# A two-layer streaming encoder step on one core: where the dense products of a head stand against the outputs of the head two back

## The chip, the cores and the metric

The program runs on one core of one Trainium2 chip. The metric is the device time of one execution in microseconds (us); the time before is the median of three runs. The profile is of one further execution.

## What is computed

The reference runs 1024 prompt frames and 32 frames of a running stream through two layers of width 1024. The change touches only the first mixer, a gated linear recurrence with 8 heads of width 128 and chunks of 64 frames:

```python
q, f, i, g = jnp.split(h @ w_in, 4, axis=-1)
forget = lbf + (1.0 - lbf) * jax.nn.sigmoid(f.astype(F32))
...
o_inter = jnp.einsum('blhk,bhkv->blhv', q * jnp.exp(b), S)
scores = jnp.einsum('btshk,bshk->bhts', decay * q[:, :, None], k)
o_intra = jnp.einsum('bhts,bshv->bthv', scores, v)
S_new = jnp.exp(b_last)[..., None] * S + jnp.einsum('bshk,bshv->bhkv', k * jnp.exp(b_last[:, None] - b), v)
...
o = rms_norm(o, g_norm) * jax.nn.silu(g.astype(F32)).reshape(B, T, A_HEADS, A_DV)
return o.reshape(B, T, D_MODEL).astype(h.dtype) @ w_out, S
```

Then x becomes x + rms_norm(mix), which is normalised again for the feed-forward part that follows.

## The kernel before

The 1056 frames are cut into three blocks of 384, 384 and 288 columns (`BL`). A block's activations lie as 8 tiles of 128 features by its columns, each split into a high and a low part (`xh`, `xl`); a weight unit of 128x1024 (`wunit`) is loaded by a DMA into `wst` (2 buffers), rounded to `wh` by ACT (L102) and its remainder put into `wl` by DVE (L103), 4 buffers each. A dense product is 24 matmuls: 8 feature tiles times three pairs of parts, in `mm_fm` (L133, weights stationary, up to 384 columns) or in `mm_tm` (L145, frames stationary, 256 columns). `mmps` gives PSUM banks from a ring of 4.

The loop over blocks b and heads h is a pipeline three units deep; a unit is one head of one block, and there are 24. In the iteration of unit c, `p1` is the unit before and `p2` the one two back. The source order of an iteration is: `stage_a` (forget and query products of c, and their evictions L756 to L764), in between them `states(p2)` (transposes `pt`, products `pu`, then the states `Sq` by DVE L947, or by ACT L945 for the first chunk); `stage_c(p1)` (the scores `psA`, `psB`, and the masked copies of them into `at`); `outputs(p2)` (the products `po`, L970 from `at` and values, L973 from `Q` and the states; then a copy and three squares on ACT into `ssq`); the list `fill[h]`; and `stage_b(c)` (the decayed products on DVE, POOL and ACT that end with `Q64` and `K64`, 2 buffers each).

In `fill`, even heads hold `vproj` (two wunits and 3 dense products for the values of a pair of heads, 72 matmuls at L145, evicted by ACT L708). Odd heads from 3 on hold `gproj` (the same for the gate of the pair whose second head `outputs` has just made: `rsqrt` of `ssq` on DVE, 10 small instructions, then the products, and evictions L725, L726, L729). At h = 1 of blocks 1 and 2 `gproj(3, b - 1)` is followed by `oback(b - 1)`, which transposes all heads' outputs (`pgt`) and splits them (L992, L993).

`fill` also advances the generators `OP[b]` by steps. A generator is `outproj` (8 steps, each one output tile `mixb`: 24 matmuls, and two scaled wunits in every second step) and then `postnorm`: step 9 is `rnorm` (one matmul pair L180, then six DVE and four ACT instructions up to `rb2`), step 10 nothing, steps 11 to 14 two feature tiles each (per tile: L243 and L244 on DVE, a square on ACT, an add into `acc` on POOL, a DMA that loads `xo` and, per step, one that stores `mixb`). For block 0 step 15 is a second `rnorm`, step 16 nothing, and steps 17 and 18 load four stored tiles each, scale them (L274) and split them (`put_x`, L209, L210). Before the change `OP[0]` stands at h = 2, 3, 4, 6 of block 1 with two steps each, and in block 2 at h = 0 (2 steps), 1 (4 steps), 4, 5, 6, 7 (one each). `OP[1]` has two steps at h = 2, 3, 4 of block 2.

Each engine has its own queue of instructions. Their order is set when the program is built: by source order, except where the builder's own estimate has a later instruction ready sooner.

Of the kernel before, what the change touches and what calls it, by code (L numbers as in the profile page):

```python
# [8 lines left out]
F32 = mybir.dt.float32  # L9
# [50 lines left out]
def build(nc, tc, I, O):  # L60
    ctx = ExitStack()
    mult, add, sub, mn = ALU.mult, ALU.add, ALU.subtract, ALU.min
# [73 lines left out]
    def mm_tm(ps, rows, units, xh, xl, t0):  # L136
        n = 24
        i = 0
        for u, (wh, wl) in enumerate(units):
            for k in range(4):  # L140
                h, l = wh[:, k * 256:k * 256 + 256], wl[:, k * 256:k * 256 + 256]
                kt = u * 4 + k
                a, b = xh[:, kt, t0:t0 + rows], xl[:, kt, t0:t0 + rows]
                for (x, w) in ((a, h), (b, h), (a, l)):
                    last_mm[0] = nc.tensor.matmul(ps[:rows, :256], x, w, start=i == 0, stop=i == n - 1)  # L145
                    i += 1
# [5 lines left out]
    def rsqrt(dst, ss, v, t, u, cnt, sq, lin):  # L152

        lin(v, ss, 1.0 / cnt, EPS)
        nc.vector.tensor_scalar(dst.bitcast(I32), v.bitcast(I32), -0.5, float(0x5f3759df), mult, add)
        sq(t, dst)
        nc.vector.tensor_tensor(t, t, v, mult)
        lin(u, t, 0.375, -1.25)
        nc.vector.tensor_tensor(t, u, t, mult)
        nc.vector.scalar_tensor_tensor(dst, t, 1.875, dst, add, mult)  # L160
        sq(t, dst)
        nc.vector.scalar_tensor_tensor(t, t, -0.5, v, mult, mult)
        nc.vector.scalar_tensor_tensor(dst, t, 1.5, dst, add, mult)
# [434 lines left out]
    V, KE = nc.vector, nc.gpsimd  # L598
# [46 lines left out]
    def run(g):  # L645
        for _ in g or ():
            pass

    def go(g, n=1):
        for _ in range(n):  # L650
            next(g, None)

    with tc.tile_pool(name="hp", bufs=1) as hp, \
# [42 lines left out]
        vts, o_raw, ssq, r_o = {}, {}, {}, {}  # L696
# [15 lines left out]
        def gproj(p, b):  # L712
            units = wpair(I["wg"], p)
            W = BL[b][1]
            ro = hp.tile([128, 6], F32, tag="ro", name="ro", bufs=2)
            nv, nt, nu = [hp.tile([128, 6], F32, tag=t, name=t, bufs=2) for t in ("nv", "nt", "nu")]
            rsqrt(ro, ssq[p, b], nv, nt, nu, 128, lambda o, x: V.tensor_tensor(o, x, x, mult),
                  lambda o, x, m, a: V.tensor_scalar(o, x, m, a, mult, add))
            for jl in range(3):
                rows = min(128, W - jl * 128)  # L720
                ps = mmps()
                mm_tm(ps, rows, units, xs[b][0], xs[b][1], jl * 128)
                sg = hp.tile([128, 256], F32, tag="sg", name="sg", bufs=2)
                rc = rts[b][:rows, jl:jl + 1]
                nc.scalar.activation(sg[:rows], ps[:rows, :256], AF.Sigmoid, scale=rc)  # L725
                V.scalar_tensor_tensor(sg[:rows], ps[:rows, :256], rc, sg[:rows], mult, mult)  # L726
                for i in range(2):
                    o = o_raw[2 * p + i, b][:rows, jl, :]
                    V.scalar_tensor_tensor(o, sg[:rows, i * 128:i * 128 + 128], ro[:rows, 3 * i + jl:3 * i + jl + 1],  # L729
                                           o, mult, mult)  # L730
# [177 lines left out]
        def states(c):  # L908

            h, b, n = c["h"], c["b"], c["n"]  # L910
            hc = (h % 2) * 128
            vt = vts[h // 2, b]
            K64 = c["K64"]
            chunks = [(q, 128, c["D128"][:, q:q + 1]) for q in range(n)]
            if b == 2:
                chunks.append((2, 32, c["D64"][:, 4:5]))
                S0 = hp.tile([128, 128], F32, tag="S", name="S", bufs=2)
                nc.sync.dma_start(S0, I["state"][h])
            pt = hps.tile([128, 512], F32, tag="hs", name="pt", bufs=1)
            kT = hp.tile([128, 3, 128], F32, tag="kT", name="kT", bufs=1)  # L920
            for (q, rows, _) in chunks:
                nc.tensor.transpose(pt[:rows, q * 128:q * 128 + 128], K64[:, q * 128:q * 128 + rows], ident)
            kTf = kT.rearrange("p a b -> p (a b)")
            nc.scalar.copy(kTf[:, :n * 128], pt[:, :n * 128])
            if b == 2:
                nc.scalar.copy(kTf[:32, 256:384], pt[:32, 256:384])
            yield
            pu = hps.tile([128, 512], F32, tag="hs", name="pu", bufs=1)
            for (q, rows, _) in chunks:
                nc.tensor.matmul(pu[:, q * 128:q * 128 + 128], kT[:rows, q], vt[:rows, q, hc:hc + 128],  # L930
                                 start=True, stop=True)
            S = state[h]
            c["S"] = before = []
            for (q, rows, dcol) in chunks:
                j = 3 * b + q
                pq = pu[:, q * 128:q * 128 + 128]
                if j == 8:
                    S = S0
                before.append(S)
                if q == 2 and j < 8:  # L940
                    new = hp.tile([128, 128], F32, tag="state", name="state", bufs=10)
                else:
                    new = hp.tile([128, 128], F32, tag="Sq", name="Sq", bufs=5)
                if j == 0:
                    nc.scalar.copy(new, pq)  # L945
                else:
                    V.scalar_tensor_tensor(new, S, dcol, pq, mult, add)  # L947
                if j == 7:
                    nc.sync.dma_start(O["st_p"][h], new)
                if j == 8:  # L950
                    nc.sync.dma_start(O["st_s"][h], new)
                S = new
            state[h] = S
# [29 lines left out]
        def oback(b):  # L983
            W = BL[b][1]
            oh, ol = os[b] = newx(b)
            for h in range(8):
                pt = hps.tile([128, 512], F32, tag="hsc", name="pgt", bufs=2)
                for jl in range(3):
                    rows = min(128, W - jl * 128)
                    nc.tensor.transpose(pt[:, jl * 128:jl * 128 + rows], o_raw[h, b][:rows, jl, :],  # L990
                                        ident[:rows, :rows])
                nc.scalar.copy(oh[:, h, :], pt[:, :W])  # L992
                V.tensor_tensor(ol[:, h, :], pt[:, :W], oh[:, h, :].bitcast(F32), sub)  # L993
# [4 lines left out]
        OP = [op0(b) for b in range(NB)]  # L998
        p1 = p2 = None
        xld = None  # L1000
        for b in range(NB):
            fill = {h: [] for h in range(8)}
            for p in range(4):
                fill[2 * p].append(lambda p=p, b=b: go(v0 if p == b == 0 else vproj(p, b), 4))
                if p < 3:
                    fill[2 * p + 3].append(lambda p=p, b=b: gproj(p, b))
            if b > 0:
                fill[1].append(lambda b=b: (gproj(3, b - 1), oback(b - 1)))
                o = OP[b - 1]
                for h in (2, 3, 4):  # L1010
                    fill[h].append(lambda o=o: go(o, 2))
                if b == 1:
                    fill[6].append(lambda o=o: go(o, 2))
            if b == 2:
                for h, n in ((0, 1), (1, 2), (4, 1), (5, 1)):
                    fill[h].insert(0, lambda n=n: go(OP[0], n))
                for h, n in ((0, 1), (1, 2), (6, 1), (7, 1)):
                    fill[h].append(lambda n=n: go(OP[0], n))
            for h in range(8):
                c = {}  # L1020
                ga = stage_a(c, h, b)
                gs = states(p2) if p2 is not None else iter(())
                go(ga)
                go(gs)
                go(ga)
                go(gs)
                if p1 is not None:
                    stage_c(p1)
                if p2 is not None:
                    outputs(p2)  # L1030
                for f in fill[h]:
                    f()
                stage_b(c)
                p2, p1 = p1, c
                if xld is not None:
                    go(xld)
                if b + 1 < NB and h == 3:
                    xld = xload(b + 1)
                    go(xld)
# [4 lines left out]
        stage_c(p1)  # L1044
        outputs(p2)
        run(states(p1))
        outputs(p1)
        gproj(3, 2)
        go(OP[1])
        oback(2)  # L1050
    mb2c, mbs[2] = pool("mb0b", "right")
# [127 lines left out]
    with tc.tile_pool(name="aps", bufs=1, space=PSUM, reuse_waits="tile") as aps:  # L1179
# [148 lines left out]
        p, o = OP[0], OP[1]  # L1328
# [134 lines left out]
```

## Time and the profile before

| | |
|---|---|
| median of 3 runs | 2586.18 us (2575.33 to 2587.52) |
| profiled execution | 2586.45 us |
| its span, first to last instruction | 2584.7 us |
| mean granted TensorE clock | 0.98 |
| busy: PE, PEld, DVE, ACT, POOL | 96%, 92%, 66%, 43%, 17% |

The first mixer's loop fills the span from about 8 us to 640 us. The iterations of block 0 start at 7.7 us, those of block 1 at 185 us, those of block 2 at 399 us; one takes 20 to 30 us. In the rows, PE is TensorE's matmuls, PEld its weight loads, SPq the queue that issues DMAs; "idle before" is the time in which an engine stood still before an instruction, and the name behind the arrow is what ended it.

### The profile page before, as it was taken

How to read it: one execution, taken by the hardware profiler on the slowest of the kernel's cores; microseconds unless marked ns; L12 is line 12 of the kernel's file. 1: busy time of each engine (PE TensorE's matmuls, PEld its weight loads, DVE VectorE, ACT ScalarE, POOL GpSimd, SP SyncE). 2: the span in 40 equal slices, each digit the busy share in tenths (PEclk: the TensorE clock that was granted, in tenths of full speed). 3: DMA queues.
4: the chain of work that ended last, by engine and by line, in shares of the span. 5: the costliest groups of instructions: out<-in, count | busy, mean ns of one | idle time of the engine just before them, and what ended most of it. 6: DMA issues, size and time to landing. Idle time of an engine off the chain costs nothing.

```text
span 2584.7 us, 44049 instructions
## 1 busy us (share of the span) xinstructions
PE 2487.6 (96%) x17124; PEld 2387.2 (92%) x17124; DVE 1704.8 (66%) x3510; ACT 1104.9 (43%) x2395; POOL 444.7 (17%) x644
## 2 busy tenths in 40 slices
PE   7999998999999999999998999989999999999997
PEld 6999998998999999999998897758899999999996
DVE  8788679787876666553467647777876666652455
ACT  6555655655543333341344324556543333342332
POOL 4443434331300000000033321111300000000021
PEclk9999999999999999999999999989999999999998
DMA  5232333433522222242455542222522222252454
GB/s 172 87 99 93 119 105 124 129 125 97 163 81 81 75 75 77 83 165 79 145 171 157 169 138 68 73 78 95 159 75 87 75 75 75 77 174 75 149 171 144
DMA packets 124153, 287.98 MB, mean 111 GB/s; under 512 B 13432, under 2 KB 68632, under 8 KB 123944
## 3 DMA queue, kind: packets, MB, share of 16 engines
q1 hardware_dynamic: 123944, 285.17, 34.6%
q8 instruction: 134, 2.20, 0.4%
q14 instruction: 75, 0.61, 0.1%
HBM read 237.25 MB, written 48.07 MB: 110 GB/s over the span
## 4 chain that ended last, share of the span: by engine, by line
PE 61%; DVE 9%; DMA 4%; ACT 3%; issue 2%; POOL 0%; SPq 0%; POOLq 0%; DVEq 0%; ACTq 0%
PE mm L133 20%; PE mm L501 15%; PE mm L410 14%; PE c L410 6%; DVE wl L103 2%; PE mm L145 2%; PE sc L1227 1%; PE pav L1285 1%; ACT wh L102 1%; DMA wst<-in_wfo 1%; PE ptp L1267 1%; DVE xl L210 1%; DMA xl<-g 1%; DVE mix L244 1%; DVE wl L99 1%
## 5 line engine op out<-in xcount | busy, mean ns | idle before, releaser
L133 PE MATMUL mm<-xh,wh 128*128 128x384 f32 (+1 forms) x1968 | 632.9, 322 | 10.7 <-ACT xh L212 7.7
L133 PE MATMUL mm<-xh,wl 128*128 128x384 f32 (+1 forms) x1968 | 626.0, 318 | 7.9 <-DVE wl L103 5.5
L133 PE MATMUL mm<-xl,wh 128*128 128x384 f32 (+1 forms) x1968 | 627.3, 319 | 2.0 <-DVE xl L213 1.7
L174 POOL TENSOR_TENSOR acc<-acc,tmp 128x384 f32<-128x384 f32 (+1 forms) x168 | 204.0, 1219 | 1737.4 <-ACT tmp L173 1734.4
L103 DVE TENSOR_TENSOR wl<-wst,wh 128x1024 fp32r<-128x1024 f32 (+1 forms) x301 | 372.9, 1241 | 174.9 <-ACT wh L102 170.7
L102 ACT CAST wh<-wst 128x1024 fp32r<-128x1024 f32 (+1 forms) x301 | 313.8, 1046 | 370.5 <-PE mm L501 213.0
L133 PEld LDWEIGHTS mm<-xh,wh 128*128 128x128 f32 x1968 | 374.0, 190 | 17.6 <-ACT xh L212 8.0
L133 PEld LDWEIGHTS mm<-xh,wl 128*128 128x128 f32 x1968 | 374.2, 190 | 17.0 <-DVE wl L103 6.6
L133 PEld LDWEIGHTS mm<-xl,wh 128*128 128x128 f32 x1968 | 373.9, 190 | 11.2 <-DVE xl L213 5.1
L501 PE MATMUL mm<-xh,wl 128*128 128x384 f32 (+1 forms) x768 | 247.8, 323 | 3.2 <-DVE wl L103 3.2
L501 PE MATMUL mm<-xh,wh 128*128 128x384 f32 (+1 forms) x768 | 247.8, 323 | 1.3 <-ACT wh L102 1.3
L501 PE MATMUL mm<-xl,wh 128*128 128x384 f32 (+1 forms) x768 | 247.6, 322 | 0.0
L145 PE MATMUL mm<-wh,xh 128*128 128x256 f32 (+1 forms) x648 | 188.6, 291 | 0.8 <-ACT vt L708 0.8
L145 PE MATMUL mm<-wh,xl 128*128 128x256 f32 (+1 forms) x648 | 185.4, 286 | 0.0
L145 PE MATMUL mm<-wl,xh 128*128 128x256 f32 (+1 forms) x648 | 184.7, 285 | 0.0
L394 ACT CAST sh<-sr 128x512 fp32r<-128x512 f32 x144 | 89.5, 622 | 172.9 <-PE mm L410 146.8
L501 PEld LDWEIGHTS mm<-xh,wl 128*128 128x128 f32 x768 | 145.2, 189 | 3.9 <-DVE wl L103 3.9
L501 PEld LDWEIGHTS mm<-xh,wh 128*128 128x128 f32 x768 | 145.4, 189 | 1.5 <-ACT wh L102 1.5
L501 PEld LDWEIGHTS mm<-xl,wh 128*128 128x128 f32 x768 | 145.3, 189 | 0.0
L145 PEld LDWEIGHTS mm<-wh,xh 128*128 128x128 f32 (+1 forms) x648 | 120.5, 186 | 3.2 <-issue 1.7
L145 PEld LDWEIGHTS mm<-wh,xl 128*128 128x128 f32 (+1 forms) x648 | 120.5, 186 | 1.1 <-issue 0.3
L145 PEld LDWEIGHTS mm<-wl,xh 128*128 128x128 f32 (+1 forms) x648 | 120.4, 186 | 0.4
(283 smaller groups left out, 5144.3 us busy)
## 6 DMA issues: line engine op xcount, KB each, us to landing
wst<-in_wfo SPq DMA_DIRECT2D x92, 512.0 KB
wst<-in_wfi SPq DMA_DIRECT2D x88, 512.0 KB
wst<-in_wfq SPq DMA_DIRECT2D x47, 512.0 KB
g<-u SPq DMA_DIRECT2D x72, 192.0 KB
wst<-in_wi SPq DMA_DIRECT2D x24, 512.0 KB
wst<-in_wg SPq DMA_DIRECT2D x24, 512.0 KB
wst<-in_wao SPq DMA_DIRECT2D x24, 512.0 KB
xl<-g SPq DMA_DIRECT2D x32, 384.0 KB
```

The source lines that it names most:

```text
L99: nc.vector.scalar_tensor_tensor(wl[:, s], st[:, s], pcol(name, k0 + k), wh[:, s].bitcast(F32), mult, sub)
L102: nc.scalar.copy(wh[:, s], st[:, s])
L103: nc.vector.tensor_tensor(wl[:, s], st[:, s], wh[:, s].bitcast(F32), sub)
L133: last_mm[0] = nc.tensor.matmul(ps[:, :W], w, x, start=i == 0, stop=i == n - 1)
L145: last_mm[0] = nc.tensor.matmul(ps[:rows, :256], x, w, start=i == 0, stop=i == n - 1)
L174: nc.gpsimd.tensor_tensor(acc[:, :W], acc[:, :W], q[:, :W], add)
L210: nc.vector.tensor_tensor(xl[:, k, :], src, xh[:, k, :].bitcast(F32), sub)
L244: nc.vector.tensor_tensor(m, m, xos[k][:, :W], add)
L394: nc.scalar.copy(h, r)
L410: last_mm[0] = nc.tensor.matmul(ps[:, :384], a, c, start=start and k == i == 0, stop=k == 3 and i == 2, skip_group_check=True)
L501: last_mm[0] = nc.tensor.matmul(ps[:, :W], a, c[:, q, :], start=start and q == i == 0, stop=stop and q == f - 1 and i == 2, skip_group_che ...
L1227: nc.tensor.matmul(pss[pr][:rows, pi, off:off + n], qts[b, g][rsl, pi, qs], kt_[rsl, g, k0:k0 + n], start=pi == 0 and off == lo, stop=samp ...
```

## The change

It moves `fill[h]` ahead of `outputs(p2)`, so `vproj` and the steps of `OP` are issued before the outputs of the unit two back. `gproj` needs those outputs; it becomes a generator that issues its two wunits and its first dense product, yields, and does `rsqrt`, the other two products and all evictions after `outputs(p2)`. `oback` stays behind `gproj`. The steps of `OP[0]` are spread anew by a table `plan` (head, number of steps, generator): in block 1 two steps at h = 2 to 6 and one at h = 7; in block 2 two at h = 0, one at h = 1, two at h = 3 and one each at h = 5 and 6. Within an iteration they now come after `vproj` and before the first product of `gproj`. `OP[1]` keeps its heads. The last `gproj(3, 2)`, behind the loop, is split in the same way.

```diff
         def gproj(p, b):
             units = wpair(I["wg"], p)
             W = BL[b][1]
-            ro = hp.tile([128, 6], F32, tag="ro", name="ro", bufs=2)
-            nv, nt, nu = [hp.tile([128, 6], F32, tag=t, name=t, bufs=2) for t in ("nv", "nt", "nu")]
-            rsqrt(ro, ssq[p, b], nv, nt, nu, 128, lambda o, x: V.tensor_tensor(o, x, x, mult),
-                  lambda o, x, m, a: V.tensor_scalar(o, x, m, a, mult, add))
             for jl in range(3):
                 rows = min(128, W - jl * 128)
                 ps = mmps()
                 mm_tm(ps, rows, units, xs[b][0], xs[b][1], jl * 128)
+                if jl == 0:
+                    yield
+                    ro = hp.tile([128, 6], F32, tag="ro", name="ro", bufs=2)
+                    nv, nt, nu = [hp.tile([128, 6], F32, tag=t, name=t, bufs=2) for t in ("nv", "nt", "nu")]
+                    rsqrt(ro, ssq[p, b], nv, nt, nu, 128, lambda o, x: V.tensor_tensor(o, x, x, mult),
+                          lambda o, x, m, a: V.tensor_scalar(o, x, m, a, mult, add))
...
+        plan = [(), [(h, 2, 0) for h in (2, 3, 4, 5, 6)] + [(7, 1, 0)],
+                [(0, 2, 0), (1, 1, 0), (2, 2, 1), (3, 2, 0), (3, 2, 1), (4, 2, 1), (5, 1, 0), (6, 1, 0)]]
         for b in range(NB):
-            fill = {h: [] for h in range(8)}
+            fill, gate = {h: [] for h in range(8)}, {}
             for p in range(4):
                 fill[2 * p].append(lambda p=p, b=b: go(v0 if p == b == 0 else vproj(p, b), 4))
                 if p < 3:
-                    fill[2 * p + 3].append(lambda p=p, b=b: gproj(p, b))
+                    gate[2 * p + 3] = gproj(p, b)
             if b > 0:
-                fill[1].append(lambda b=b: (gproj(3, b - 1), oback(b - 1)))
...
+                gate[1] = gproj(3, b - 1)
+            for h, n, o in plan[b]:
+                fill[h].append(lambda o=o, n=n: go(OP[o], n))
...
                 if p1 is not None:
                     stage_c(p1)
+
+                for f in fill[h]:
+                    f()
+                go(gate.get(h, iter(())))
                 if p2 is not None:
                     outputs(p2)
-                for f in fill[h]:
-                    f()
+                run(gate.get(h))
+                if b > 0 and h == 1:
+                    oback(b - 1)
                 stage_b(c)
...
+        gt = gproj(3, 2)
+        go(gt)
         outputs(p1)
-        gproj(3, 2)
+        run(gt)
```

## Rows read from the trace of the kernel before

**Rows 1.** The page: engines' busy time, and one of the costliest groups.

```profile
PE 2487.6 (96%) x17124; PEld 2387.2 (92%) x17124; DVE 1704.8 (66%) x3510; ACT 1104.9 (43%) x2395; POOL 444.7 (17%) x644
...
L174 POOL TENSOR_TENSOR acc<-acc,tmp 128x384 f32<-128x384 f32 (+1 forms) x168 | 204.0, 1219 | 1737.4 <-ACT tmp L173 1734.4
```

**Rows 2.** PE's waits from 0 to 760 us: total, times, longest.

```profile
PE po L973 <- DVE Sq L947: 9.4, 7, 2.7
...
PE pt L922 <- POOL K L905: 4.2, 2, 2.4
PE mm L133 <- DVE wl L103: 3.6, 1, 3.6
...
PE po L973 <- ACT Sq L945: 3.3, 1, 3.3
```

**Rows 3.** Timeline of PE in two iterations (start, length, instruction).

```profile
108.43 0.80 PE L973 MATMUL po<-Sq,Q 128*128 128x128 f32 x2 [3.27 <-ACT Sq L945]
...
411.89 0.80 PE L973 MATMUL po<-Sq,Q 128*128 128x128 f32 x2 [2.43 <-DVE Sq L947]
412.48 1.49 PE L180 MATMUL mm<-acc,ones 128*128 128x384 f32 x2
413.20 0.99 PE L145 MATMUL mm<-wh,xh 128*128 128x256 f32 x1
```

**Rows 4.** Stretches: length, busy time (instructions) by engine, PE's granted clock, DMA.

```profile
83.36:93.21 9.85, 9.85 (x84) 9.85 (x83) 8.64 (x25) 5.77 (x21) 9.69 (x17) 1.00 0.29 98
104.45:120.63 16.18, 12.91 (x84) 12.53 (x83) 11.73 (x38) 9.06 (x25) 8.56 (x16) 0.79 0.28 77
...
333.77:346.63 12.86, 10.60 (x86) 10.22 (x85) 12.52 (x47) 6.27 (x22) 7.39 (x14) 1.00 0.27 85
...
408.08:422.67 14.59, 12.16 (x89) 11.20 (x87) 12.08 (x44) 8.84 (x25) 5.35 (x16) 0.88 0.24 74
431.69:443.06 11.37, 10.34 (x87) 10.15 (x86) 10.19 (x34) 9.00 (x27) 11.06 (x21) 1.00 0.59 199
443.06:460.95 17.89, 13.78 (x133) 12.63 (x131) 17.07 (x53) 8.92 (x21) 2.92 (x7) 0.90 0.29 89
...
545.12:560.94 15.82, 13.11 (x86) 11.79 (x85) 13.14 (x57) 7.40 (x24) 6.52 (x18) 0.78 0.25 79
570.15:580.46 10.31, 10.31 (x86) 9.63 (x85) 9.10 (x42) 5.32 (x23) 4.93 (x16) 1.00 0.25 81
```

**Rows 5.** The same view: all iterations from the third on.

```profile
47.28:599.98 552.70, 531.80 (x4832) 514.93 (x4831) 442.03 (x1341) 315.98 (x811) 222.50 (x443) 0.98 0.35 110
```

**Rows 6.** Timeline of DVE in block 2, heads 5 and 6.

```profile
545.61 0.92 DVE L274 SCALAR_TENSOR_TENSOR xo<-xo,pv,rb 128x384 f32<-128x384 f32 x1 [1.24 <-DMA xo<-xsa]
546.46 0.45 DVE L762 TENSOR_TENSOR tmp<-mm,rb 128x288 f32<-128x288 f32 x1
...
548.37 0.33 DVE L947 SCALAR_TENSOR_TENSOR Sq<-state,D,pu 128x128 f32<-128x128 f32 x1
...
580.02 0.38 DVE L811 TENSOR_TENSOR Q<-ZZ,D 128x80 f32<-128x80 f32 x2
```

**Rows 7.** Timeline of DVE in block 2, heads 0 to 2.

```profile
420.59 0.55 DVE L163 SCALAR_TENSOR_TENSOR rb<-tmp,rb 128x384 f32<-128x384 f32 x1
...
421.21 0.61 DVE L243 SCALAR_TENSOR_TENSOR mixb<-mixb,pv,rb 128x384 f32<-128x384 f32 x1
...
422.43 0.55 DVE L244 TENSOR_TENSOR mixb<-mixb,xo 128x384 f32<-128x384 f32 x1
...
446.64 1.22 DVE L103 TENSOR_TENSOR wl<-wst,wh 128x1024 fp32r<-128x1024 f32 x1
```

**Rows 8.** Timeline of PE behind the loop.

```profile
610.93 0.36 PE L145 MATMUL mm<-wh,xh 128*128 128x256 f32 x1
...
613.41 1.12 PE L930 MATMUL pu<-vt,kT 128*128 128x128 f32 x6
```

**Rows 9.** Timeline of the DMA queue in block 2, head 1.

```profile
423.00 2.01 SPq L227 DMA_DIRECT2D xo<-in_x  x2
```

More of the change, by code (lines that the diff above doesn't have):

```diff
@@ L1005, in build @@
                 if p < 3:
-                    fill[2 * p + 3].append(lambda p=p, b=b: gproj(p, b))
+                    gate[2 * p + 3] = gproj(p, b)
             if b > 0:
-                fill[1].append(lambda b=b: (gproj(3, b - 1), oback(b - 1)))
[L1009 to L1018, printed above, removed]
+                gate[1] = gproj(3, b - 1)
+            for h, n, o in plan[b]:
+                fill[h].append(lambda o=o, n=n: go(OP[o], n))
             for h in range(8):
```

## The prediction

> **What bounds the kernel now.** I read the busy shares first. PE is busy for 2487.6 us of 2584.7 and the weight loads that run under it for 92% [rows 1]; no other engine is near that. PE's sequence of matmuls sets the end, and a change of order that leaves the work as it is can gain only what PE stands idle, and what it loses to the clock behind that. So the second view is PE's waits. Up to 760 us they hold 12.7 us in front of one instruction, the output product L973, which waits for the states (9.4 us for DVE L947, 3.3 us for ACT L945), and 3.6 us in front of a dense product that waits for the low part of a weight unit, DVE L103 [rows 2]. The rest of the 2584.7 us can't be touched by this diff.
>
> The third view measures what these waits cost with the clock. Each stretch of rows 4 runs from the first output product of an iteration to the end of the 72 gate or value matmuls behind it. Undisturbed it takes 9.85 us in block 0 and at most 10.31 us later, at a granted clock of 1.00. In block 0, head 4, it takes 16.18 us: 3.27 us of wait [rows 3], and a mean clock of 0.79, which means the 1.2 GHz level instead of 2.4 GHz in 42% of it, or (1 - 0.79) x 16.18 = 3.4 us lost. PE had stood idle just before the clock fell. Two more stretches show the same, at 0.88 and 0.78 [rows 4].
>
> The surplus of each, against 9.85 or 10.31 us:
> block 0 head 4: 16.18 - 9.85 = 6.33;
> block 1 head 5: 12.86 - 10.31 = 2.55;
> block 2 head 0: 14.59 - 10.31 = 4.28, less the 0.72 us from the `rnorm` pair L180 to the next product [rows 3], which is work, = 3.56;
> block 2 head 1: 11.37 - 10.31 = 1.06;
> block 2 head 5: 15.82 - 10.31 = 5.51.
> Together 19.0 us. The waits in these five are 3.3, about 2.5, 2.4, about 1.1 and 2.7 us [rows 2 to 4]; that leaves 0.7 of the 12.7 us for short ones elsewhere. The pool in front of the outputs is 19.7 us.
>
> A second pool is the stretch from `oback(1)` to the first output product of block 2, head 2: 17.89 us at a clock of 0.90 [rows 4], with the 3.6 us wait for L103 in it [rows 2]. The clock costs 0.10 x 17.89 = 1.8 us, so 5.4 us could go.
>
> **The change part by part.** *Order of products and outputs.* No instruction is added. Behind `stage_c`, PE now finds 72 value matmuls in even iterations, or 24 gate matmuls in odd ones, before `po`. How long is that cover? (9.85 - about 1 for eight small output matmuls) / 3 = 3.0 us for 24, and 8.8 us for 72. In the tail 19 of them take 613.41 - 610.93 = 2.5 us, which gives 3.1 for 24 [rows 8]. The waits it must hide are 3.3 us and 2.4 us in even iterations and up to 2.7 us in odd ones [rows 2, 3]. All fit; the tightest, head 5 of block 2, by only 0.3 us. Are the weights there? In all undisturbed stretches the 72 products follow the outputs without a gap, and no row of PE's waits names their weights (L145 isn't among the causes above 1 us), so a start some 1 to 6 us earlier should find them. I take the whole 19.7 us. The bounds are 19.7 and, where each of the four long waits (3.3, 2.7, 2.5, 2.4) forms again in front of another product, 19.7 - 10.9 = 8.8.
>
> What is late next? `po` ends 3 to 9 us later (up to 17 us where `OP` products stand between), and behind it ACT's copy and squares, then `rsqrt` and the gate's evictions. PE next needs them through the PSUM ring, two products of the following iteration later. DVE and ACT have their queue in front of that; DVE is busy for 442.03 of 552.70 us in the loop, 80%, and 83% if 19 us leave it [rows 5]. So something will form again: PE arrives earlier everywhere while DVE's chain is as long as before. I charge 4.0 us for this, between 0 and the 10.9 us above, near the low end because the undisturbed iterations show the ring and the scores without waits; the only other wait of size is 4.2 us in two places for POOL's K [rows 2].
>
> *Steps of `OP[0]`.* A step pair of `outproj` (k = 6, 7) moves from head 6 to head 5 of block 1: the same 48 matmuls, two wunits with their DMAs, and evictions. `rnorm` moves from block 2 to block 1, head 6: one L180 pair, four ACT and six DVE instructions, the last of them L163 with 0.55 us [rows 7], so at most 3.3 us of DVE. Of the eight `postnorm` tiles, each 0.61 + 0.55 = 1.16 us of DVE [rows 7], an ACT square, a POOL add of 1.2 us [rows 1], an `xo` load and half a store, two go to block 1 head 7, four to block 2 head 0 and two stay in head 1. Before, DVE ran most of the eight inside head 1, next to `oback`. There it was late with the weight split: L103 starts at 446.64 [rows 7], 3.6 us after PE began the transposes at 443.06 [rows 4], and PE waits about as long for it. With about five tiles fewer in front of it, 5.8 us, the split is done before PE comes. But DVE enters head 1 later relative to PE, since PE gains 3.56 us in head 0 and DVE doesn't. That leaves 2 us of the 5.8, against a wait of 3.6 us. I take 3.5 of the 5.4 us, the bounds being 0 and 5.4.
>
> On SP's queue the `xo` loads stood in head 1 between weight loads (two issues in 2.0 us [rows 9]); they now stand in heads 7 and 0, where the next weight load is behind them by as much. Its cover is the two units already split in the four buffers. If that is gone, one weight unit is late by about 2 us. The second `rnorm` (head 4 to 3) and the two rewrites (heads 6 and 7 to 5 and 6) cost as before; they are hidden by DVE's free time, 110 us in the loop [rows 5]. The tail gains nothing: 19 of 24 gate products stand before `pu` already [rows 8].
>
> *Sum:* -19.7 - 3.5 + 4.0 = -19.2 us. Against the profiled execution, 2586.45 us: 2567.2 us. That execution is within 0.3 us of the median of the runs shown (2586.18), so the median should be 2567 as well; one of those three runs was 11 us lower, and the lower end of the range has to allow for such a one.
>
> **The rivals.** *A. Waits form again on DVE.* For it speaks the way DVE's queue holds things up: at 545.61 it stands 1.24 us until the load for L274 has landed, and the eviction L762 and the state L947, which PE then waited for, come behind it [rows 6]. Such rewrites now fall into heads 5 and 6, and four tiles into head 0. Against it: 17% of DVE's time stays free. If the 10.9 us form again and the `OP` steps gain nothing, the gain is 8.8 us: 2577.6 us.
> The Trainium skill, "TensorE: Matmul & The Clock Gate", section on engine queue depths, states that ACT's and DVE's queues are strictly first in, first out. The trace agrees in [rows 6]; by that rule alone, work that PE is given sooner doesn't shorten the chain ahead of L947, and A is what follows.
>
> *B. The order doesn't matter.* The builder's estimate already moves products forward, as in the tail [rows 8]; it could leave the outputs where they were. Against it: in every stretch of rows 4 the outputs came first, as in the source, so the source order does decide. Then 2586 us, or 2583 with the `OP` steps alone.
>
> *C. The later outputs hold `Q64`.* `stage_b` writes the buffer of `Q64` that `po` two units back reads. In head 6 of block 2 DVE writes it at 580.02 [rows 6], and `po` would now run at 570.15 + 8.8 = 579, so the write comes to wait for it in even iterations. If weight splits stand behind that write (DVE L811 0.4 us and the rest of the level about 0.7 us, then L103 1.22 us [rows 6, 7]), PE waits about 2.3 us in each of 11 iterations, and with a fall of the clock like that of head 0 (3.56 - 2.4 = 1.2 us) 3.5 us: 38.5 - 19.2 = +19 us, 2605 us. It decides from (19.2 + 12.9) / 11 = 2.9 us an iteration. Against it: the splits are made two units ahead.
>
> **How the numbers follow.** Forecast 0.64 (2567, own range 2557 to 2574), A 0.18 (2578), B 0.08 (2586), C 0.10 (2605). What this kernel's measurement can tell from no change is about 0.5%, 12.9 us. Faster by more than that takes the forecast and a little of A: 0.67. Within it lie the rest of A, B and a weak C: 0.24. Slower by more: 0.09. The range reaches down to 2556, all 25.1 us of both pools gone and 5 us more, towards the lowest of the runs, and up to 2584, so that B and C are left out.
>
> **What would show it.** Right: PE's waits for L947 and L945 in front of `po` fall from 12.7 us to under 2; the five stretches stay near 10 us at a clock of 1.00; the wait for L103 falls under 1 us; in the timeline 72 or 24 products at L145 stand before the first `po`; the loop's end, now about 640 us, comes at about 620. Wrong, for A: the same total under other names (evictions, `pu`, scores). For B: `po` still before the products. For C: DVE or ACT idle before `Q` at L811 or L807, released by `po`, and PE waiting for L103.

## The result, and the profile after

The changed kernel takes 2563.79 us (median of 5 runs, 2561.34 to 2566.91) against 2584.07 us for the kernel before in the same runs: a ratio of 0.9928, interval 0.9915 to 0.9941. By the ratio that is 18.6 us less (15.2 to 22.0); the medians differ by 20.3. The forecast was 19.2 us less. The profiled span falls from 2584.7 to 2562.0 us. The last transposes `pgt` of the first mixer start at 637.06 us before and at 617.90 us after: 19.2 us of those 22.7 are won there; the other 3.5 lie behind it, where the two kernels have the same source.

The page's busy line answers to [rows 1]: PE is busy for 12.4 us less with the same number of instructions, 9.3 us of it up to the last `pgt` and 3.1 behind it. Fewer of them run at the lower clock: its mean is 0.984 where it was 0.980.

```profile
PE 2475.2 (97%) x17124; PEld 2375.9 (93%) x17124; DVE 1714.7 (67%) x3510; ACT 1102.5 (43%) x2395; POOL 451.9 (18%) x644
```

PE's waits from 0 to 760 us in the changed kernel (total, times, longest), for [rows 2]:

```profile
PE pgt L992 <- DVE xl L995: 4.8, 2, 3.3
PE pu L932 <- ACT kT L926: 3.6, 2, 2.3
...
PE pt L924 <- POOL K L907: 3.2, 2, 2.6
...
PE po L975 <- DVE Sq L949: 1.4, 1, 1.4
```

The 12.7 us in front of `po` are 1.4 us, and the 3.6 us for L103 are gone. New are 3.6 us of `pu` behind ACT's copy `kT` (in the states of block 0 head 5 and block 2 head 1), and 3.3 us in `oback(1)`.

The stretches that answer to [rows 4], each from the first gate or value product to the end of the 72 and the outputs, then `oback(1)` with the products of head 2, and the loop of [rows 5] (length, busy time and instructions by engine, PE's granted clock, DMA):

```profile
103.08:113.28 10.20, 10.20 (x87) 10.07 (x85) 8.35 (x24) 5.83 (x15) 8.83 (x17) 1.00 0.38 125
335.58:346.12 10.54, 10.54 (x91) 10.51 (x90) 9.33 (x31) 7.51 (x19) 2.31 (x2) 1.00 0.30 101
398.74:408.55 9.81, 9.81 (x87) 9.65 (x85) 9.81 (x23) 5.23 (x14) 9.34 (x16) 1.00 0.60 204
417.50:420.90 3.40, 3.13 (x46) 2.87 (x46) 1.83 (x3) 1.26 (x4) 0.76 (x2) 0.50 0.83 281
421.56:433.33 11.77, 10.38 (x86) 10.12 (x85) 10.72 (x36) 6.42 (x22) 7.68 (x18) 1.00 0.38 126
433.33:449.11 15.78, 12.38 (x133) 11.39 (x132) 15.28 (x51) 11.64 (x29) 3.86 (x11) 1.00 0.22 67
533.28:543.60 10.32, 10.32 (x87) 9.65 (x85) 9.79 (x51) 5.87 (x21) 4.37 (x14) 1.00 0.43 120
47.28:588.10 540.82, 528.20 (x4862) 512.98 (x4860) 457.20 (x1356) 314.63 (x815) 228.66 (x442) 1.00 0.36 114
```

Four of the five stretches take 9.8 to 10.5 us at full clock, with no idle time; they took 12.9 to 16.2 us. The fifth, block 2 head 1, is no shorter (11.77 against 11.37). The loop's row ends at the first score matmul behind the last head, which stood at 605.43 us before; that is 17.3 us earlier ([rows 5] ends 5.4 us short of that point). DVE is busy for 457.20 of its 540.82 us, 85%, where 83% was forecast.

The order is the one forecast: in block 0 head 4 the products at L145 begin at 103.08, and the outputs come 72 matmuls later without a wait:

```profile
103.08 0.39 PE L145 MATMUL mm<-wh,xh 128*128 128x256 f32 x1
...
111.81 0.60 PE L972 MATMUL po<-vt,at 128*128 128x128 f32 x4
```

What is left of the waits shows in PE's timeline of block 2, heads 0 to 2 (start, length, instruction, idle before and releaser):

```profile
417.77 1.65 PE L932 MATMUL pu<-vt,kT 128*128 128x128 f32 x6 [2.27 <-ACT kT L926]
...
427.19 0.49 PE L975 MATMUL po<-Sq,Q 128*128 128x128 f32 x2 [1.39 <-DVE Sq L949]
```

and ACT's timeline tells why `kT` was late:

```profile
413.09 0.31 ACT L863 COPY at<-psB 64x192 f32<-64x192 f32 x1 [3.36 <-DVE at L860]
413.31 2.00 ACT L102 CAST wh<-wst 128x1024 fp32r<-128x1024 f32 x2
...
415.57 0.45 ACT L978 COPY oraw<-po 128x384 f32<-128x384 f32 x1
...
417.26 0.46 ACT L926 COPY kT<-pt 128x384 f32<-128x384 f32 x1
```

PE has made the transposes `pt` by 412.3, but ACT stands 3.36 us for DVE's masked copy L860, then works off two weight casts, the output copy and the three squares of L983, and only then copies `kT`. The later outputs have moved their ACT work in front of `kT`. That is rival A in one place: 2.27 us of idle time, and 3.4 us of half clock, in which up to 1.7 us are lost.

### The profile page after: what moved, and what is told of

Read it like the earlier page. It is cut to its first block, busy times and chain, and to the rows that moved or that the text cites. A ratio compares the mean times of both kernels' runs of the same rounds, so it can differ in the third digit from the quotient of the medians.

```text
span 2562.0 us, 44049 instructions
## 1 busy us (share of the span) xinstructions
PE 2475.2 (97%) x17124; PEld 2375.9 (93%) x17124; DVE 1714.7 (67%) x3510; ACT 1102.5 (43%) x2395; POOL 451.9 (18%) x644
## 4 chain that ended last, share of the span: by engine, by line
PE 73%; DVE 13%; DMA 5%; ACT 4%; issue 3%; POOL 1%; SPq 0%; POOLq 0%; DVEq 0%; ACTq 0%
PE mm L133 25%; PE mm L501 16%; PE mm L410 14%; PE c L410 6%; PE mm L145 5%; DVE wl L103 2%; PE sc L1231 1%; ACT wh L102 1%; PE pav L1289 1%; PE ptp L1271 1%; DMA xl<-g 1%; DMA wst<-in_wfq 1%; DVE mixb L244 1%; DMA wst<-in_wfo 1%; DVE xl L210 1%
## 5 line engine op out<-in xcount | busy, mean ns | idle before, releaser
L133 PE MATMUL mm<-xh,wh 128*128 128x384 f32 (+1 forms) x1968 | 633.1, 322 | 10.5 <-ACT xh L212 7.5
L103 DVE TENSOR_TENSOR wl<-wst,wh 128x1024 fp32r<-128x1024 f32 (+1 forms) x301 | 373.1, 1244 | 154.5 <-ACT wh L102 153.5
L145 PE MATMUL mm<-wh,xh 128*128 128x256 f32 (+1 forms) x648 | 186.7, 288 | 0.8 <-ACT vt L708 0.8
L145 PE MATMUL mm<-wh,xl 128*128 128x256 f32 (+1 forms) x648 | 183.4, 283 | 0.0
L145 PE MATMUL mm<-wl,xh 128*128 128x256 f32 (+1 forms) x648 | 182.9, 282 | 0.0
L145 PEld LDWEIGHTS mm<-wh,xh 128*128 128x128 f32 (+1 forms) x648 | 118.1, 182 | 3.5 <-ACT vt L708 0.8
L145 PEld LDWEIGHTS mm<-wh,xl 128*128 128x128 f32 (+1 forms) x648 | 118.2, 182 | 0.7
L145 PEld LDWEIGHTS mm<-wl,xh 128*128 128x128 f32 (+1 forms) x648 | 118.3, 183 | 0.5
```

Source lines behind the costliest of these rows:

```text
L103: nc.vector.tensor_tensor(wl[:, s], st[:, s], wh[:, s].bitcast(F32), sub)
L133: last_mm[0] = nc.tensor.matmul(ps[:, :W], w, x, start=i == 0, stop=i == n - 1)
```

## The experiments

All ratios are to the kernel before. The changed kernel was run once more, unaltered, beside some of them:

> The changed kernel once more, unaltered, on the chip of the kernels of this call, as their measure. Every theory: its ratio of 0.9928 to the kernel before, within 0.0015.

2561.75 us, ratio 0.9930 [0.9918, 0.9942]: the result stands. Its trace tells how far a single trace can be trusted. The last `pgt` come 18.8 us earlier than before (19.2 in the first trace), but head 1 of block 2 takes 31.15 us from score to score, where the first trace of the same kernel has 28.22. The difference is the clock: in the second trace the wait of 3.26 us in `oback(1)` comes with 6.8 us at 0.50,

```profile
439.03:445.86 6.83, 5.91 (x26) 5.80 (x27) 5.18 (x12) 1.96 (x5) 0.00 (x0) 0.50 0.51 142
```

and in the first the stretch around it stays at 1.00. So a difference of some 3 us in one place between two traces need not come from an edit.

### The order alone, and the steps of `OP` alone

```diff
-        plan = [(), [(h, 2, 0) for h in (2, 3, 4, 5, 6)] + [(7, 1, 0)],
-                [(0, 2, 0), (1, 1, 0), (2, 2, 1), (3, 2, 0), (3, 2, 1), (4, 2, 1), (5, 1, 0), (6, 1, 0)]]
+        plan = [(), [(2, 2, 0), (3, 2, 0), (4, 2, 0), (6, 2, 0)],
+                [(0, 2, 0), (1, 4, 0), (2, 2, 1), (3, 2, 1), (4, 1, 0), (4, 2, 1), (5, 1, 0), (6, 1, 0), (7, 1, 0)]]
```

> The new order alone: dense products ahead of the outputs, while the steps of OP stand at the heads where they stood before. Theory (the gain is PE's idle time in front of the outputs with the clock behind it, 19.7 us, and belongs to the order): 2568 us, ratio 0.9935, no wait over 1 us in front of the output products, the weight wait behind oback in block 2 still there or longer. Rival (the spread of the residual's steps over more heads is what lets PE run on, and without it the same waits form again on DVE and ACT in block 2): 2577 us or more, ratio 0.997.

Within an iteration the steps come behind `vproj` here; before the change some of them, in heads 0, 1, 4 and 5 of block 2, stood ahead of the other work of `fill`.

2578.62 us, ratio 0.9982 [0.9970, 0.9994]: 4.6 us of gain instead of the 16 that the sum's terms give. The waits for `po` are gone. Up to the first scores of block 2 head 1 this kernel is as far as the changed one (417.97 us against 419.35 and, before, 430.15). Then the time is lost: from there to the scores of head 3 it takes 65.86 us, where the kernel before takes 57.13 (430.15 to 487.28) and the changed one 56.07. Windows of the order alone:

```profile
417.97:483.83 65.86, 58.53 (x456) 53.79 (x455) 53.92 (x158) 34.15 (x96) 24.54 (x48) 0.84 0.39 124
432.50:453.00 20.50, 15.17 (x74) 12.34 (x74) 17.78 (x52) 6.66 (x16) 3.66 (x7) 0.50 0.35 107
```

and of the changed kernel:

```profile
419.35:475.42 56.07, 51.29 (x456) 49.00 (x455) 44.76 (x143) 35.02 (x94) 19.63 (x46) 0.99 0.37 121
```

The second window of the order alone is 20.5 us at the 1.2 GHz level throughout, and 8.9 of the 9.8 us between the two long stretches lie in the iteration of head 2 (36.75 against 27.85 us from score to score).

The counterpart is the kernel before with the new `plan` for `OP` and the old order:

```diff
-                o = OP[b - 1]
-                for h in (2, 3, 4):
-                    fill[h].append(lambda o=o: go(o, 2))
...
+            for h, n, o in plan[b]:
+                fill[h].append(lambda o=o, n=n: go(OP[o], n))
```

> The new heads for the steps of OP alone, in the order of before: outputs ahead of the dense products. Theory: 3.5 us of the gain, 2582 us, ratio 0.9986; the waits in front of the output products stay near 12 us in all, the weight wait of 3.6 us behind oback goes. Rival: most of the gain, 2572 us or less, ratio 0.995.

2584.50 us, ratio 1.0005 [0.9993, 1.0017]: nothing. PE's waits there are those of [rows 2], with L103 shortened from 3.6 to 2.3 us:

```profile
PE po L973 <- DVE Sq L947: 10.1, 9, 2.4
...
PE po L973 <- ACT Sq L945: 3.3, 1, 3.3
...
PE mm L133 <- DVE wl L103: 2.3, 1, 2.3
```

So one part is worth 4.6 us, the other nothing, and both together 18.6: the parts don't add. The `OP` steps are worth 14.0 us (18.6 - 4.6) once the order is new.

### What in the steps of `OP`: the tiles, or the norm ahead of them

Five kernels keep the new order and move only steps of `OP[0]`. All eight `postnorm` tiles in block 2 head 1, `rnorm` left in block 1 head 6:

```diff
-        plan = [(), [(h, 2, 0) for h in (2, 3, 4, 5, 6)] + [(7, 1, 0)],
-                [(0, 2, 0), (1, 1, 0), (2, 2, 1), (3, 2, 0), (3, 2, 1), (4, 2, 1), (5, 1, 0), (6, 1, 0)]]
+        plan = [(), [(h, 2, 0) for h in (2, 3, 4, 5, 6)],
+                [(1, 4, 0), (2, 2, 1), (3, 2, 0), (3, 2, 1), (4, 2, 1), (5, 1, 0), (6, 1, 0)]]
```

> The changed kernel, with all eight residual tiles of block 0 in head 1 of block 2 as before the change; everything else of the new order and the new table stays. The order alone had lost some 13 us against the changed kernel, at heads 1 and 2 of block 2. Theory (the eight tiles beside oback in one iteration hold up DVE and ACT, and the product and the outputs no longer wait there as one long stop but in many small ones, at 1.2 GHz): those 10 us or more come back, 2574 us, clock of 1.2 GHz for over 10 us in that stretch. Rival (the loss came from the place of the second rnorm, the rewrites or output tiles k = 6, 7): within 3 us of the changed kernel, 2564 to 2567 us.

2566.12 us, ratio 0.9947 [0.9934, 0.9959]. And the same with `rnorm` in block 2 head 0 as well, which is the only difference between the two:

```diff
-        plan = [(), [(h, 2, 0) for h in (2, 3, 4, 5, 6)],
-                [(1, 4, 0), (2, 2, 1), (3, 2, 0), (3, 2, 1), (4, 2, 1), (5, 1, 0), (6, 1, 0)]]
+        plan = [(), [(h, 2, 0) for h in (2, 3, 4, 5)],
+                [(0, 2, 0), (1, 4, 0), (2, 2, 1), (3, 2, 0), (3, 2, 1), (4, 2, 1), (5, 1, 0), (6, 1, 0)]]
```

> The changed kernel with the second-block rnorm back at block 2 head 0 and all eight postnorm tiles at head 1, the other steps of OP at their new heads. Theory: rnorm at head 0 on top of eight tiles in head 1 makes DVE so late that the builder moves head 2's dense products behind transposes and outputs, as in the kernel with the new order alone: 1.2 GHz for about 20 us and 2576 to 2578 us, ratio 0.997. Rival: the loss with the new order alone came from the heads of the two rewrites or of steps 6 and 7; then this is like the kernel with eight tiles in head 1 alone, about 2566 us, ratio 0.995.

2575.79 us, ratio 0.9977 [0.9965, 0.9988], as with the order alone. One moved `rnorm` costs 0.0030 of 2582 us by the ratios, 7.7 us, and their intervals don't touch. That is the larger part of the 14.0 us. With all eight tiles issued in head 1 and `rnorm` early, the kernel is 4.4 to 4.9 us behind the two measurements of the changed one by the ratios, with intervals that overlap (though its five runs all lie above the five of the second measurement beside it), and 1.7 us behind it at the last `pgt` by the trace. The other moved steps, by the ratios 0.9977 and 0.9982, are worth 1.3 us, within the noise. In the traces the last `pgt` of the mixer start at about 620 us in the first and 632 in the second, 12 us apart.

The tiles themselves show the reason. DVE's busy time and instructions at L243, the first instruction of a tile, with the tiles issued in head 1 and `rnorm` early:

```profile
370.00:395.00 25.00, 2.72 (x4) 1.00 0.38 122
395.00:417.00 22.00, 2.46 (x4) 1.00 0.52 170
417.00:435.00 18.00, 0.00 (x0) 1.00 0.44 149
```

and with `rnorm` in head 0:

```profile
370.00:395.00 25.00, 0.00 (x0) 1.00 0.29 92
395.00:417.00 22.00, 0.00 (x0) 1.00 0.40 128
417.00:435.00 18.00, 5.73 (x8) 0.91 0.39 132
```

Where a tile is issued decides little about when it runs: the builder moves all eight forward, some of them by 40 us, once `rb2` is there, and the changed kernel, which issues them in three heads, has the same four and four. With the norm in head 0, DVE's last instruction of `rb2` (L163) starts at 416.52 us, and all eight stand in one stretch behind it. DVE's groups in 417 to 435 us of that kernel (busy us, mean ns):

```profile
L244 DVE TENSOR_TENSOR mixb<-mixb,xo 128x384 f32<-128x384 f32 x8 | 6.2, 782 | 0.0
L243 DVE SCALAR_TENSOR_TENSOR mixb<-mixb,pv,rb 128x384 f32<-128x384 f32 x8 | 5.7, 726 | 0.0
```

where the changed kernel has in the same stretch

```profile
L103 DVE TENSOR_TENSOR wl<-wst,wh 128x1024 fp32r<-128x1024 f32 x3 | 4.0, 1325 | 2.5 <-ACT wh L102 2.5
```

Eight tiles take 11.9 us of the 18, and no weight split is among them. The splits for the products of head 2 come at 446 us, though ACT had rounded both units by 419.3, so no load and no cast held them up. ACT and DVE of that kernel:

```profile
418.27 1.05 ACT L102 CAST wh<-wst 128x1024 fp32r<-128x1024 f32 x1
...
446.13 1.22 DVE L103 TENSOR_TENSOR wl<-wst,wh 128x1024 fp32r<-128x1024 f32 x1
```

PE's timeline of that kernel shows what stands there instead:

```profile
431.61 0.59 PE L133 MATMUL mm<-xh,wh 128*128 128x288 f32 x1
431.99 0.44 PE L133 MATMUL mm<-xl,wh 128*128 128x288 f32 x1
...
437.82 0.66 PE L992 MATMUL pgt<-ident,oraw 128*128 128x128 f32 x3 [2.77 <-DVE xl L995]
438.27 1.06 PE L932 MATMUL pu<-vt,kT 128*128 128x128 f32 x4
...
443.99 1.89 PE L992 MATMUL pgt<-ident,oraw 128*128 128x128 f32 x6 [1.29 <-DVE xl L995]
...
447.41 0.61 PE L133 MATMUL mm<-xh,wl 128*128 128x288 f32 x1 [0.34 <-DVE wl L103]
```

Four of the 48 dense matmuls of head 2 are among the transposes, outputs and states of that stretch; the other 44 wait until the split is done and then start at half clock. In the changed kernel the `pgt` and `pt` stand among all 48, which are done before `pu`. The Trainium skill, "TensorE: Matmul & The Clock Gate", in its paragraph on engine queue depths, says that DVE takes its queue strictly first in, first out; the trace agrees, in that the splits, whose inputs were there at 419.3, start at 446 behind the tiles and other work. That `rnorm`'s place costs the time is shown by the two kernels; that it does so by way of the tiles in front of the splits is read from the traces, and no run takes it apart further.

Three more spread the tiles differently with `rnorm` early. Two tiles in each of four heads, block 1 heads 6 and 7 and block 2 heads 0 and 1, or one head later:

```diff
-        plan = [(), [(h, 2, 0) for h in (2, 3, 4, 5, 6)] + [(7, 1, 0)],
-                [(0, 2, 0), (1, 1, 0), (2, 2, 1), (3, 2, 0), (3, 2, 1), (4, 2, 1), (5, 1, 0), (6, 1, 0)]]
+        plan = [(), [(h, 2, 0) for h in (2, 3, 4, 5)] + [(6, 3, 0), (7, 1, 0)],
+                [(0, 1, 0), (1, 1, 0), (2, 2, 1), (3, 2, 0), (3, 2, 1), (4, 2, 1), (5, 1, 0), (6, 1, 0)]]
```

> The changed kernel, with two residual tiles in each of four iterations: heads 6 and 7 of block 1, heads 0 and 1 of block 2 (changed kernel: 0, 2, 4, 2). Theory (what counts is the most that DVE gets in one iteration): the kT wait of 2.3 us at head 0 to 1 and the wait of 1.4 us for a state go, 4 us faster than the changed kernel, 2560 us. Rival (the earlier tiles make the weight split for head 0 late, as with four tiles in head 7): no faster, 2564 us or more.

```diff
-                [(0, 2, 0), (1, 1, 0), (2, 2, 1), (3, 2, 0), (3, 2, 1), (4, 2, 1), (5, 1, 0), (6, 1, 0)]]
+                [(0, 1, 0), (1, 1, 0), (2, 1, 0), (2, 2, 1), (3, 2, 0), (3, 2, 1), (4, 2, 1), (5, 1, 0), (6, 1, 0)]]
```

> The same, with two tiles each at head 7 of block 1 and heads 0, 1 and 2 of block 2. Theory as for two each from head 6: 4 us faster than the changed kernel, 2560 us; the last two tiles stand in an iteration that has 8 us more of PE's work to hide them. Rival (the first output tile of block 1 waits for the one mixb buffer until the last two tiles are stored): PE waits for PSUM in head 2, no faster than 2564 us.

2563.30 us, 0.9935 [0.9922, 0.9947], and 2563.44 us, 0.9935 [0.9922, 0.9949]: no gain over the changed kernel. Tiles 2, 4, 2 in block 1 heads 6 and 7 and block 2 head 0:

```diff
-        plan = [(), [(h, 2, 0) for h in (2, 3, 4, 5, 6)] + [(7, 1, 0)],
-                [(0, 2, 0), (1, 1, 0), (2, 2, 1), (3, 2, 0), (3, 2, 1), (4, 2, 1), (5, 1, 0), (6, 1, 0)]]
+        plan = [(), [(h, 2, 0) for h in (2, 3, 4, 5, 7)] + [(6, 3, 0)],
+                [(0, 1, 0), (2, 2, 1), (3, 2, 0), (3, 2, 1), (4, 2, 1), (5, 1, 0), (6, 1, 0)]]
```

> The changed kernel with two of block 0's residual tiles each taken out of heads 0 and 1 of block 2 and put into heads 6 and 7 of block 1 (then 2, 4 and 2 tiles at heads 6, 7 and 0). Theory (what is left in block 2 at heads 0 and 1, some 7 us of PE waits for kT, for a state and for oback and 1.7 us of clock, is DVE's and ACT's backlog from the tiles): the waits there fall to 3 us, 5 us faster than the changed kernel, 2559 us. Rival (DVE is full wherever the tiles stand, so the same waits form in block 1): no faster than the changed kernel, 2564 us or more.

2572.23 us, 0.9954 [0.9940, 0.9968], with this among PE's waits:

```profile
PE mm L133 <- DVE wl L103: 7.5, 2, 5.9
```

5.9 us of it lie in block 2 head 0 (at 396 us), where the changed kernel has no such wait. With two tiles each in heads 6 and 7 of block 1, a wait of 2.8 us for a split stands there (at 394 us). That the four tiles of block 1 head 7 hold this split up is likely; no run takes it apart.

### One stall brought back

```diff
+                if (b, h) == (0, 4):
+                    outputs(p2)
                 for f in fill[h]:
                     f()
                 go(gate.get(h, iter(())))
-                if p2 is not None:
+                if p2 is not None and (b, h) != (0, 4):
                     outputs(p2)
```

> The changed kernel, with the outputs ahead of the value products again in block 0 head 4 alone. Theory (a wait in front of the outputs reaches the end with its clock): the wait of 3.3 us and a clock of about 0.8 in that stretch come back, 16 us instead of 10, and the kernel is 5 to 6 us slower than the changed one, 2569 us. Rival (PE only waits there instead of later, since the engines behind it set the pace): the stretch is longer, later waits are shorter by as much, 2564 us.

2570.76 us, 0.9953 [0.9939, 0.9967], 6.5 us above the changed kernel by the ratios (0.0025 of 2582; the intervals just overlap). PE's timeline and the window behind it:

```profile
108.33 0.49 PE L975 MATMUL po<-Sq,Q 128*128 128x128 f32 x2 [3.53 <-ACT Sq L947]
```

```profile
109.20:112.60 3.40, 3.15 (x14) 3.15 (x15) 3.40 (x15) 1.85 (x9) 3.16 (x10) 0.50 0.70 257
```

and, for comparison, the half clock behind the same stall in the kernel before:

```profile
107.55:114.38 6.83, 5.95 (x26) 5.76 (x27) 6.83 (x24) 4.04 (x16) 5.59 (x13) 0.50 0.58 155
```

The iteration takes 27.62 us from score to score instead of 23.31. That is 4.3 us, where the prediction had priced the stall at 6.33. The wait is as long as before (3.53 against 3.27 us), but the half clock is 3.4 us long instead of 6.8, and the wait of 1.32 us for `kT` that the changed kernel has in the next iteration is gone. Another 3.7 us come between heads 1 and 2 of block 2 (31.87 against 28.22), where nothing was edited; the unaltered kernel's second trace has 31.15 there, so these don't count for the stall.

### How much product stands ahead of the outputs in odd heads

None (the gate's generator yields first):

```diff
         def gproj(p, b):
+            yield
             units = wpair(I["wg"], p)
...
-                    yield
```

> The changed kernel, but the gate's generator yields before its first product, so that in odd iterations nothing stands between the scores and the outputs (vproj and the OP steps stay ahead of the outputs). Theory: the 24 gate products of odd iterations hide the waits that the kernel before had there (about 2.5 us in block 1 head 5, 1.1 in block 2 head 1, 5.5 with the clock in block 2 head 5), so they come back: about 8 us slower than the changed kernel, ratio to before near 0.996, and PE's waits in front of the output products rise from 1.4 us to about 6. Rival: the OP steps or the even iterations carry the gain and the first gate product hides nothing: as fast as the changed kernel, ratio 0.993.

2566.53 us, 0.9946 [0.9928, 0.9963], and the mixer ends 6.5 us later in the trace; the interval of the ratio overlaps the changed kernel's. The waits for `po` are back, 7.2 us of them, but 2.7 us in block 0 head 5, 3.5 in block 2 head 1 and 0.9 in block 1 head 7:

```profile
128.70 0.49 PE L975 MATMUL po<-Sq,Q 128*128 128x128 f32 x2 [1.76 <-ACT Sq L947]
...
130.33 0.49 PE L975 MATMUL po<-Sq,Q 128*128 128x128 f32 x2 [0.92 <-DVE Sq L949]
...
432.28 0.79 PE L975 MATMUL po<-Sq,Q 128*128 128x128 f32 x2 [2.09 <-DVE Sq L949]
```

In block 1 head 5 and block 2 head 5, where the kernel before had stood for 2.3 and 2.7 us, PE doesn't wait. The theory's sum of the waits is near (7.2 us, 6 said), but of its three places only block 2 head 1 is right: with head 4 of block 0 no longer late, head 5 is. In block 1 head 5 the 48 matmuls of `outproj` now stand ahead of the outputs (327.15 to 335.58 us in the changed kernel) and hide more than the gate product does. What removed the wait in block 2 head 5 stays open; the steps of `OP` alone won 2.6 of the 5.5 us there.

Two products ahead:

```diff
-                ps = mmps()
-                mm_tm(ps, rows, units, xs[b][0], xs[b][1], jl * 128)
                 if jl == 0:
+                    pss = [mmps(), mmps()]
+                    for i in range(2):
+                        mm_tm(pss[i], 128, units, xs[b][0], xs[b][1], i * 128)
                     yield
...
+                if jl == 2:
+                    pss.append(mmps())
+                    mm_tm(pss[2], rows, units, xs[b][0], xs[b][1], jl * 128)
+                ps = pss[jl]
```

> The changed kernel with two gate products of an odd iteration ahead of the outputs instead of one. Theory: what waits are left in front of an output (1.4 us in block 2 head 1) go, and nothing else changes: 0 to 2 us faster than the changed kernel, ratio to before 0.992 to 0.993. Rival: two of the four PSUM banks are then held until rsqrt, which stands behind the outputs' squares, so the third product or the next forget product waits for a bank, and the kernel is 3 us slower or more, with new waits in front of products at L145 or L133.

2560.67 us, 0.9915 [0.9900, 0.9931]. The wait for `po` is gone, and waits of 1.9 us each for a weight split and for `at` have come. It is the lowest median here, 3 us under the changed kernel, but the intervals overlap. No dense product waits for one of the four banks of `mmps`; the wait for `at` is one of `pgt`, which shares two other banks with the scores that the masked copies read.

### A third buffer for `Q64`

```diff
-            c["K4"], c["K16"], c["K64"], c["Q64"] = K4, K16, K64, Q64 = ht("K4"), ht("K16", 1), ht("K64"), ht("Q64")
+            c["K4"], c["K16"], c["K64"], c["Q64"] = K4, K16, K64, Q64 = ht("K4"), ht("K16", 1), ht("K64"), ht("Q64", 3)
```

> The changed kernel with three buffers for Q64 instead of two, so that no write of Q has to wait for the outputs of the unit two back. Theory: DVE waits only 0.3 us for an output in the changed kernel's trace, so this is worth nothing: within 1.5 us of the changed kernel, ratio 0.993. Rival (the later outputs hold Q64, in part): some microseconds faster, ratio 0.991 or lower.

2568.15 us, 0.9946 [0.9931, 0.9961]: slower than the changed kernel, if anything. Here is DVE in block 0 head 4 of the changed kernel:

```profile
116.76 2.36 DVE L103 TENSOR_TENSOR wl<-wst,wh 128x1024 fp32r<-128x1024 f32 x2 [0.64 <-ACT wh L102]
119.03 0.42 DVE L813 TENSOR_TENSOR Q<-ZZ,D 128x96 f32<-128x96 f32 x2
```

and with the third buffer:

```profile
115.84 0.42 DVE L813 TENSOR_TENSOR Q<-ZZ,D 128x96 f32<-128x96 f32 x2
...
117.20 2.36 DVE L103 TENSOR_TENSOR wl<-wst,wh 128x1024 fp32r<-128x1024 f32 x2 [0.48 <-ACT wh L102]
```

With two buffers the builder puts the two splits in front of the write of `Q64` that has to wait for the outputs; with three it puts them behind. Later, in the first products of block 2 head 1, PE waits 3.1 us for a split.

## Why the prediction was right, and where its steps were not

**The total.** 19.2 us were forecast, 18.6 measured. The signs named for it came, but for one of the five stretches (11.77 us, block 2 head 1): `po` waits under 2 us (1.4), no wait above 1 us for L103, products ahead of `po`, and an end of the loop's last transposes at 618 us where about 620 was said.

**The order's 19.7 us.** Taken from score to score, the iterations with the five stalls became 4.75 us shorter (block 0 head 4; 6.33 forecast), 2.72 (block 1 heads 5 and 6 together; 2.55), 1.45 (block 2 head 0; 3.56), 1.04 (head 1; 1.06, and 3.5 more for the `OP` steps) and 5.50 (head 5; 5.51). The last is exact. The stall brought back shows what is right and wrong in the price of a single one: the idle time is (3.53 us), but the clock behind it was priced at 3.4 us and cost 1.7, and with the 1.32 us for `kT` that went the iteration lost 4.3 us and not 6.33. What is missing in the first, third and fourth came back as waits: 1.32 us for `kT` in block 0 head 5, 2.27 us for it with the 3.4 us of half clock in block 2 head 1, 1.39 us at `po`, 3.26 us at `pgt`.

**New waits, 4.0 us.** The forecast less the measured cuts of the five, (6.33 + 2.55 + 3.56 + 4.56 + 5.51) - (4.75 + 2.72 + 1.45 + 1.04 + 5.50) = 22.5 - 15.5 = 7.0 us, is what came back in this trace, so this term was mis-sized: 7.0 in place of 4.0. In the second trace of the same kernel the cuts are 13.0 us, and 9.5 came back. The other side is that 3.7 us were won where 0.7 us were forecast, 1.8 us of them in the tail ("the tail gains nothing"), where the transposes wait 0.60 us for POOL's `K` instead of 1.83, and 1.9 us in other iterations. The two errors, 3.0 us each, cancel (about 5 us each in the second trace), so that the total came within 0.6 us of the forecast is luck.

**The `OP` steps, 3.5 us.** The step that failed is the treatment of this term as one of its own that adds to the others. It measured nothing alone and 14.0 us on top of the order. The prediction counted tiles in front of a split in head 1; the runs show that the number issued there is the smaller part (0.9947 with eight), and that the place of `rnorm` is the larger, 7.7 us, as the builder moves tiles forward once their norm is ready. The prediction gave `rnorm` at most 3.3 us of DVE; what it left out is that `rnorm` frees 11.9 us of tiles at one moment.

**Rival A** is what the order alone would have been: 4.6 us of gain, less than the 8.8 given for it. The forecast of 16 us for that half was wrong, and the result is near the forecast because the other half removes most of the waits and the slow clock that the first makes. That the two parts make up the sum is luck too. **B** is refuted by the order in the timeline, by the 18.6 us and by the stall brought back. **C** didn't come: the condition that it named, splits behind the write of `Q64`, is what the builder avoids with two buffers.

## What to carry to other kernels

A stall in front of a small dependent product costs its idle time and, in these traces, some slow clock behind it, of 3.4 to 6.8 us at half speed for the same stall; independent products issued ahead of it win both, less the waits that form elsewhere. Undo it in one place to have the price. Two edits to one pipeline should be run one at a time as well as together: here 4.6 and 0 made 18.6. Where a builder or scheduler moves work forward by itself, ask for each group when its last input becomes ready, not where it is issued: the norm ahead of eight tiles counted for more than the heads of the tiles. And a buffer that takes a wait away changes an order too; here it brought a new wait of 3.1 us and no gain.

## What the runs showed of the hardware

The length of a single wait did not tell whether the clock fell. In the changed kernel PE stood 3.26 us in `oback(1)` and the stretch of 433.33 to 449.11 stayed at a granted clock of 1.00, while 2.27 us in front of `pu` came with 3.4 us at 0.50. In a second execution of the same kernel the same wait of 3.26 us came with 6.8 us at 0.50 (439.03 to 445.86). So a sum that charges the clock for each stall by one trace can be off by some microseconds per stall. In the order alone, no wait in 432.5 to 453 is longer than 2.6 us and PE is busy for 15.17 of 20.50 us, but the clock is 0.50 from end to end. At most half of the 15.17 us, 7.6, is lost by that (an estimate from the busy time), where the one long wait of [rows 3] was followed by 6.8 us at 0.50 and a loss of 3.4.
